# A decoder block's front: token rows summed at written-out points, a fourth place for split rows, and the final roots spread a step later

## The chip, the cores and the metric

The kernel runs on one core of a Trainium2 chip. The time is device microseconds of one execution, the median of the runs shown. The engines of a core work side by side, each in the order of its own queue: TensorE (PE, matrix products), VectorE (DVE), ScalarE (ACT), GpSimd (POOL) and SyncE (SP), whose queue issues nearly all transfers between the chip's memory and the core's.

## The reference

One layer on x of 2048 tokens by 1024 channels, in float32:

```
hn  = RMSNorm(x) * norm1_g
u_pool | q | k | v = hn @ W_in             # 512 channels each
y   = pool mixer(u_pool)                   # window means 2, 4, 8, 16, minus u; a 128x128 product each
o   = stick-breaking attention(q, k, v)    # 8 heads of 64 channels, causal
h   = x + [RMSNorm(y), RMSNorm(o)] @ W_out
h   = h + relu(RMSNorm(h) @ W_up)^2 @ W_down
out = RMSNorm(h) * final_g
```

## The kernel before

Channels lie on the 128 partitions, tokens along the free dimension, in four tiles of 512 tokens (`NT = 4`). To keep float32 accuracy every operand of a large product is split in a high and a low part (`split`, L150 and L151: ACT writes the rounded high part, DVE the rest), and each product is three matmuls (L182 to L184: high by high, high by low, low by high).

The kernel has a front (norm 1, input projection, pool mixer, attention), the output projection, the up projection and the down projection; the last two use a Strassen-like scheme with fewer block products. `front(q)` treats tiles 2q and 2q + 1, called a and b. It writes a program: steps (`in_proj`, one step for 128 output channels of one tile, 24 matmuls) and notes (Python calls between the steps). Output channels 0 to 3 are the pool groups, 4 to 7 q, 8 to 11 k, 12 to 15 v. In q = 0, tile 0's first ten projections come first, then six channel blocks for tiles 0 and 1 in turn with the same weights, then tile 1's last ten. Attention (`near`, units of two blocks of 128 queries) is spread among the steps.

Small work waits in a first-in first-out list, `later`. After each step `run` takes one or more entries of it (`catch_up`), and a note can empty it. What an entry issues on an engine is put behind certain earlier instructions of that engine, the last split of weights and the evacuation before the last. The instructions of each engine are otherwise ordered by a planner that runs when the kernel is built, with modelled times: ready work can be put ahead of work written earlier.

Norm 1 of tile 0 sums squares over the transposed tile. For tiles 1 to 3 (`norm1_rms(j)`) four blocks of 128 token rows of x, 128x1024 each, are loaded into a single buffer, tag `xr` in pool `pa`, and squared in place by ACT, which also accumulates each row's sum into `sums1`. Load and squares are entries of `later`; then come the inverse root on POOL and its spread over the partitions (`to_all`: eight matmuls at L248, a copy by ACT). For tile 1 the note stands before the fourth projection of tile 0, for tile 2 at the start of the shared blocks, for tile 3 at the start of q = 1.

The ring with the tag `st` (three places) holds split rows on their way to memory: `pls` (pool differences), `qk`, `vt` (v, transposed) and `mix` (the normed outputs). A place is free once its store has landed, or for `pls` once its matmuls are done. The constant tile `rlast`, 4 KB on each partition, holds two spread roots of norm 2, written in the up projection.

The down projection ends with the product P3, in two halves of eight steps, `kk` 0 to 7. Between steps the final norm of finished token tiles is done: `final_root` takes the means (eight matmuls at L210, a DVE instruction at L218) and makes the root on POOL, `yr`, in some 15 small instructions; `final_put` spreads it by eight matmuls (L248), ACT copies it, DVE multiplies eight chunks (L1403) and SP stores them (L1404). In the second half the steps 6 and 7 are held back for `last_steps`, which finishes the last token tile (stores at L1458).

Of the kernel before, what the change touches and what calls it, by code (L numbers as in the profile page):

```python
# [8 lines left out]
F32 = mybir.dt.float32  # L9
F32R = mybir.dt.float32r  # L10
# [5 lines left out]
P = 128  # L16
# [29 lines left out]
def hymba_block(ctx: ExitStack, tc: tile.TileContext, xT, x_rows, gains, w_in, pool_w, w_out, w_up, w_down, out):  # L46
# [259 lines left out]
        return (hpb if j % 2 else hpa).tile([P, 2, T], F32R, tag="h", name="h", align_bytes=256)  # L306

    def make_st():
        return pa.tile([P, 2, T], F32R, tag="st", name="mix", align_bytes=256, bufs=3)


    pw = []
# [15 lines left out]
    def note(emit):  # L328
        prog.append((0, emit, False))
# [39 lines left out]
    def norm1_first():  # L369
# [10 lines left out]
            ss = sum_squares([x[:, k] for k in range(KD)])  # L380
        st[0]["r"] = inv_rms(ss, D, root_tile(), nc.vector)

    def norm1_rms(j):
        got = st[j]["ss"] = sums1[:, j - 1]
        t = {}

        def load(b):
            t[b] = pa.tile([P, D], F32, tag="xr", name="xr", bufs=1)
            nc.sync.dma_start(t[b], x_rows[j, b])

        def square(b):
            nc.scalar.activation(t[b], t[b], AF.Square, accum_out=got[:, b:b + 1])
            if b + 1 < TB:
                load(b + 1)
        later.append(lambda: load(0))
        later.extend(lambda b=b: square(b) for b in range(TB))
        later_rms(st[j], "r", lambda: st[j]["ss"], D, lambda: root_tile() if j == 2 else None, j == 1)

    def norm1(j):
# [14 lines left out]
    def pool_group(j, g, ps):  # L414
        w = WINDOWS[g]
        if g == 0:
            st[j]["y"] = pa.tile([P, 4, T], F32, tag="yb", name="yb", bufs=1)
        u = pa.tile([P, PAD + T], F32, tag="u", name="u")
        nc.gpsimd.tensor_copy(u[:, 0:PAD], carry[:, g])
        if j == 0:  # L420
            took = nc.vector.tensor_tensor(u[:, PAD:], ps, st[0]["r"], ALU.mult)
        else:
            took = nc.scalar.activation(u[:, PAD:], ps, AF.Copy)
        nc.gpsimd.tensor_copy(carry[:, g], u[:, T:T + PAD])
        pl = pa.tile([P, T], F32, tag="ev", name="pl")
        if w == 2:
            nc.vector.tensor_tensor(pl, u[:, PAD - 1:PAD + T - 1], u[:, PAD:], ALU.subtract)
            if j == 0:
                nc.vector.tensor_tensor(pl[:, 0:1], u[:, PAD:PAD + 1], u[:, PAD:PAD + 1], ALU.subtract)
        else:  # L430
            sums = pa.tile([P, PAD + T], F32, tag="s", name="s")
            if w == 4:
                pair = pa.tile([P, PAD + T], F32, tag="s", name="s")
                nc.vector.tensor_tensor(pair[:, PAD - 2:], u[:, PAD - 2:], u[:, PAD - 3:PAD + T - 1], ALU.add)
                nc.vector.tensor_tensor(sums[:, PAD:], pair[:, PAD:], pair[:, PAD - 2:PAD + T - 2], ALU.add)
            else:
                nc.vector.tensor_tensor_scan(sums[:, PAD:], u[:, PAD:], u[:, PAD - w:PAD + T - w], window_sum[:, g:g + 1],
                                             op0=ALU.add, op1=ALU.subtract)
                if j < NT - 1:
                    nc.vector.tensor_reduce(window_sum[:, g:g + 1], u[:, PAD + T - w:], axis=mybir.AxisListType.X, op=ALU.add)  # L440
            nc.vector.scalar_tensor_tensor(pl, sums[:, PAD:], 1.0 / w, u[:, PAD:], op0=ALU.mult, op1=ALU.subtract)
            if j == 0:
                nc.vector.tensor_tensor(pl[:, 0:w - 1], sums[:, PAD:PAD + w - 1], recip[:, 0:w - 1], ALU.mult)
                nc.vector.tensor_tensor(pl[:, 0:w - 1], pl[:, 0:w - 1], u[:, PAD:PAD + w - 1], ALU.subtract)
        d = pa.tile([P, 2, T], F32R, tag="st", name="pls", align_bytes=256, bufs=3)
        split((d[:, 0], d[:, 1]), pl)
        pp = psx.tile([P, T], F32, tag="px", name="pp")
        nc.tensor.matmul(pp, pw[0][:, 0, g], d[:, 0], start=True, stop=False)
        nc.tensor.matmul(pp, pw[0][:, 0, g], d[:, 1], start=False, stop=False)
        nc.tensor.matmul(pp, pw[0][:, 1, g], d[:, 0], start=False, stop=True)  # L450
        nc.scalar.activation(st[j]["y"][:, g], pp, AF.Copy, scale=gs[:, g:g + 1])
        return took
# [16 lines left out]
        normed(4, part, g, make_st, lambda: st[j]["rm"], mx[j][at:at + 4])  # L469

    def keep_qk(j, c, dst, ps):
        d = pa.tile([P, 2, T], F32R, tag="st", name="qk", align_bytes=256, bufs=3)
        if j == 0:
            t = pa.tile([P, T], F32, tag="ev", name="qkr")
            nc.vector.tensor_tensor(t, ps, st[0]["r"], ALU.mult)
            ps = t
        took = split((d[:, 0], d[:, 1]), ps)
        for e in range(2):
            for x in range(2):
                nc.sync.dma_start(dst[2 * c + e][j][x * DH:(x + 1) * DH].bitcast(F32),  # L480
                                  d[e * DH:(e + 1) * DH, x].bitcast(F32))
        return took

    def keep_v(j, c, ps):
        vf = pa.tile([P, T], F32, tag="ev", name="vf")
        if j == 0:
            took = nc.vector.tensor_tensor(vf, ps, st[0]["r"], ALU.mult)
        else:
            took = nc.scalar.activation(vf, ps, AF.Copy)
        pt = psx.tile([P, TB, 2, DH], F32, tag="px", name="ptv")  # L490
        for b in range(TB):
            nc.tensor.transpose(pt[:, b], vf[:, b * P:(b + 1) * P], ident)
        vt = pa.tile([P, 2, TB, 2, DH], F32R, tag="st", name="vt", align_bytes=256, bufs=3)
        split((vt[:, :, :, 0], vt[:, :, :, 1]), pt.rearrange("p b e d -> p e b d"))
        for e in range(2):
            nc.sync.dma_start(vs[2 * c + e][j].bitcast(F32),
                              vt[:, e].rearrange("p b x d -> p (b x d)").bitcast(F32))
        return took
# [47 lines left out]
    def front(q):  # L546


        a, b = 2 * q, 2 * q + 1

        def rate(i):
            note(lambda: state.update(ratio=RATIO_FRONT[3 * q + i]))
        rate(0)
        if q == 0:
            note(start)
            note(norm1_first)
            note(pool_weights)
        else:
            note(lambda: (load_x(b, bigp), norm1_rms(b), norm1(b), pace(2)))
        for i, c in enumerate((EARLY if q else FIRST) + POOL):  # L560
            if q == 0 and i == 2:
                note(lambda: load_x(b, x0p))
            if q == 0 and i == 3:
                note(lambda: norm1_rms(b))
            if q == 0 and i == 4:
                note(lambda: (catch_up(len(later)), norm1(b)))
            if q == 0 and i == 8:
                note(lambda: (catch_up(len(later)), to_att(), load_x(b + 1, bigp)))
                attend(a, 0)
                attend(a, 1)  # L570
            in_proj(a, c)
            if q and i in (2, 5):
                attend(a, i // 3)
        note(lambda: (catch_up(len(later)), pool_norm(a)))
        rate(1)
        for h2 in (2, 3):
            note(lambda h2=h2: (norm1_rms(2) if h2 == 2 else None) if q == 0 else attn_norm(0) if h2 == 2 else None)
            for c in range(4 + h2, 16, 4):
                in_proj(a, c)
                in_proj(b, c, True)  # L580
            attend(a, h2)
            attend(b, h2)
        note(lambda: (catch_up(len(later)), (load_acc(0), load_mix(0, KD), attn_norm(1)) if q else norm1(b + 1), pace(1)))
        rate(2)
        for i, c in enumerate(EARLY + POOL if q else POOL + EARLY):
            if q == 0 and i == 4:
                note(lambda: pool_norm(b))
            if q == 0 and i == 6:
                note(lambda: pace(2))
            if q and i == len(EARLY):  # L590
                note(lambda: (catch_up(len(later)), pace(1)))
            in_proj(b, c)
            if i in ((2, 5) if q else (6, 9)):
                attend(b, i // 3 % 2 if q else i // 9)
        note(lambda: (catch_up(len(later)), (pool_norm(b), catch_up(len(later))) if q else None))
# [596 lines left out]
    def down(pools):  # L1192
# [320 lines left out]
        for g, (n_, i, kk, qs_) in enumerate(steps):  # L1513
# [26 lines left out]
            if n_ == "P3":  # L1540
                if qs_ == (1,):
                    free = 0
                if kk in (0, 2) and finals:
                    final_root(*finals.pop(0))
                elif kk in (1, 3) and roots:
                    final_put(*roots.pop(0))
                elif kk == 4 and qs_ == (1,):
                    last_turn()
        last_steps(held, PAIRS[1][0])
# [175 lines left out]
```

## Time and profile before

| | us |
|---|---|
| runs | 1877.05, 1880.71, 1885.54 |
| median | 1880.71 |
| profiled execution, its time | 1885.53 |
| profiled execution, its span from the first to the last instruction | 1883.8 |

The mean granted TensorE clock over the span is 0.995 of full speed. The profile is that of one execution; it names instructions by line, engine and tile, says how long each engine was busy, and puts each idle time of an engine down to what ended it.

### The profile page before, as it was taken

To read this page: it belongs to the slowest core of one execution; us is meant where nothing else is said; L and a number is where in the kernel's file an instruction comes from. 1 tells how busy PE (TensorE), PEld (TensorE's weight loads), DVE (VectorE), ACT (ScalarE), POOL (GpSimd) and SP (SyncE) were. 2 spreads that over 40 slices of the span, in tenths; PEclk is the share of its full clock that TensorE was granted. 3 is DMA by queue.
4 is the path that set the end of the run, shared out by engine and by line. 5 is a ranking of instruction groups with operands and counts; after the bars stand their busy time and mean duration, and the time that the engine had idled before them with its cause. 6 is when DMAs were issued, how large, how long until landed. Compare 5 with 4: busy or idle time off the path is not lost.

```text
span 1883.8 us, 26602 instructions
## 1 busy us (share of the span) xinstructions
PE 1861.4 (99%) x8859; PEld 1550.8 (82%) x8859; DVE 1457.0 (77%) x2100; ACT 1027.4 (55%) x1620; POOL 224.5 (12%) x466
## 2 busy tenths in 40 slices
PE   9999999999999999999999999999999999999997
PEld 7888878888888888888888888887888888888887
DVE  6977779677865977887799988886665677988774
ACT  6655667465544455555567555554332665656543
POOL 1222124122311040000000000000010010020110
PEclk9999999999999999999999999999999999999999
DMA  8876796899797868988798988889999899999862
GB/s 271 265 270 201 234 301 223 258 326 303 261 360 256 297 215 293 344 281 309 277 347 304 320 293 284 287 301 337 370 328 329 276 318 305 331 298 347 288 212 92
DMA packets 223892, 542.20 MB, mean 288 GB/s; under 512 B 26240, under 2 KB 32384, under 8 KB 219904
## 3 DMA queue, kind: packets, MB, share of 16 engines
q1 hardware_dynamic: 218992, 531.75, 81.2%
q0 software_dynamic: 4608, 8.39, 2.5%
q8 instruction: 72, 1.18, 0.3%
q14 instruction: 76, 0.62, 0.1%
q10 hardware_dynamic: 144, 0.26, 0.0%
HBM read 355.75 MB, written 184.55 MB: 287 GB/s over the span
## 4 chain that ended last, share of the span: by engine, by line
PE 79%; DMA 8%; DVE 7%; issue 2%; ACT 2%; POOL 1%; SPq 1%; DVEq 0%; ACTq 0%; POOLq 0%
PE pb L1349 16%; PE pY L1176 16%; PE pb L1527 12%; PE pZ L1176 8%; PE pd L182 6%; PE pd L183 6%; PE pd L184 6%; PE pX L1176 4%; PE po L730 1%; PE pta L718 1%; DVE hl L151 1%; DMA raw<-in_w_in_dram 1%; DMA t<-in_w_down_dram 1%; DMA sr<-su 1%; DMA h<-mx 1%
## 5 line engine op out<-in xcount | busy, mean ns | idle before, releaser
L1176 PE MATMUL pY<-sa,hw 128*128 128x512 f32 x1536 | 365.7, 389 | 0.8 <-ACT u L1099 0.7
L1176 PEld LDWEIGHTS pY<-sa,hw 128*128 128x128 f32 x1536 | 288.0, 188 | 61.8 <-ACT u L1099 1.3
L1349 PE MATMUL pb<-ad,wd 128*128 128x512 f32 x1344 | 305.1, 389 | 0.2 <-DVE ad L151 0.2
L182 PE MATMUL pd<-h,hl 128*128 128x512 f32 x752 | 296.9, 395 | 3.8 <-DVE qk L151 3.8
L183 PE MATMUL pd<-h,hl 128*128 128x512 f32 x752 | 296.6, 394 | 0.0
L184 PE MATMUL pd<-h,hl 128*128 128x512 f32 x752 | 296.0, 394 | 0.0
L1349 PEld LDWEIGHTS pb<-ad,wd 128*128 128x128 f32 x1344 | 252.2, 188 | 53.0 <-DVE ad L151 0.6
L1527 PE MATMUL pb<-ad,wd 128*128 128x512 f32 x1104 | 253.6, 390 | 1.4 <-ACT ad L150 1.3
L1527 PEld LDWEIGHTS pb<-ad,wd 128*128 128x128 f32 x1104 | 206.6, 188 | 44.8 <-ACT ad L150 1.8
L151 DVE TENSOR_TENSOR ad<-ar,ad 128x1024 fp32r<-128x1024 f32 x160 | 194.1, 1220 | 42.6 <-ACT ad L150 42.0
L150 ACT ACTIVATE ad<-ar 128x1024 fp32r<-128x1024 f32 x160 | 168.9, 1057 | 90.2 <-PE pb L1349 25.2
L1176 PE MATMUL pZ<-sa,hw 128*128 128x512 f32 x768 | 185.7, 389 | 0.0
L150 ACT ACTIVATE hl<-raw 128x512 fp32r<-128x512 f32 x168 | 104.0, 629 | 119.6 <-PE pd L184 73.2
L1176 PEld LDWEIGHTS pZ<-sa,hw 128*128 128x128 f32 x768 | 144.1, 188 | 29.8
L182 PEld LDWEIGHTS pd<-h,hl 128*128 128x128 f32 x752 | 141.9, 189 | 31.3 <-DVE qk L151 4.2
L184 PEld LDWEIGHTS pd<-h,hl 128*128 128x128 f32 x752 | 141.9, 189 | 28.4
L151 DVE TENSOR_TENSOR hl<-raw,hl 128x512 fp32r<-128x512 f32 x168 | 114.5, 687 | 65.6 <-ACT hl L150 65.1
L183 PEld LDWEIGHTS pd<-h,hl 128*128 128x128 f32 x752 | 142.0, 189 | 26.4
L151 DVE TENSOR_TENSOR hw<-rt,hw 128x512 fp32r<-128x512 f32 x128 | 86.5, 684 | 33.6 <-ACT hw L150 33.5
L150 ACT ACTIVATE wd<-wq 128x1024 fp32r<-128x1024 f32 x56 | 59.5, 1063 | 79.3 <-PE pb L1349 70.4
L151 DVE TENSOR_TENSOR wd<-wq,wd 128x1024 fp32r<-128x1024 f32 x56 | 68.4, 1222 | 37.3 <-ACT wd L150 35.8
L1093 ACT ACTIVATE a<-a 128x512 f32<-128x512 f32 x96 | 60.0, 629 | 65.4 <-DVE a L1135 29.3
(235 smaller groups left out, 2688.8 us busy)
## 6 DMA issues: line engine op xcount, KB each, us to landing
ar<-sd SPq DMA_DIRECT2D x96, 512.0 KB, 5.9
ar<-sdi SPq DMA_DIRECT2D x64, 512.0 KB, 5.7
rb<-in_w_up_dram SPq DMA_DIRECT2D x30, 1024.0 KB, 6.5
sd<-a SPq DMA_DIRECT2D x104, 256.0 KB, 5.1
raw<-in_w_in_dram SPq DMA_DIRECT2D x50, 512.0 KB, 4.6
sdi<-hr SPq DMA_DIRECT2D x96, 256.0 KB, 5.4
wr<-in_w_down_dram SPq DMA_DIRECT2D x48, 512.0 KB, 5.6
sd<-s SPq DMA_DIRECT2D x88, 256.0 KB, 4.6
```

What stands on the lines that cost most here:

```text
L150: nc.scalar.activation(hi, src, AF.Copy)
L151: return nc.vector.tensor_tensor(lo, src, hi.bitcast(F32), ALU.subtract)
L182: nc.tensor.matmul(ps, hl[:, 0, c], hi, start=(k == 0), stop=False)
L183: nc.tensor.matmul(ps, hl[:, 0, c], lo, start=False, stop=False)
L184: last_mm[0] = nc.tensor.matmul(ps, hl[:, 1, c], hi, start=False, stop=(k == n - 1))
L718: nc.tensor.transpose(pt[:, x * P:(x + 1) * P], sg[:, x * P:(x + 1) * P], ident)
L730: nc.tensor.matmul(po[0:m, p * 256 + to:p * 256 + to + hi - lo], vw[:, 2 * p + v, 0:m], at[:, x, lo:hi], start=(p == 0 and n == 0), skip_g ...
L1093: nc.scalar.activation(t, src, AF.Relu)
L1176: nc.tensor.matmul(t, w[:, wx, c], a[:, ax, c % 2], start=first and c == 0 and x == 0, stop=last and c == G - 1 and x == 2, skip_group_che ...
L1349: nc.tensor.matmul(b, t[:, wx, 2 * (kk % 2) + c, i * P:(i + 1) * P], a[:, ax, c], start=p in ("P1", "P5", "P2") and kk == 0 and c == 0 and ...
L1527: nc.tensor.matmul(ps[q, n], block(t, wx, c, n), left_[q][:, ax, c], start=(n_ in ("P1", "P3") and kk == 0 and c == 0 and x == 0), stop=(n ...
```

## The change

Four edits. The ring `st` gets a fourth place. The token rows' buffer `xr` goes; `rlast` takes its part. Loads and squares are written out by a generator, `row_sums`, in five parts per tile (load 0; square 0 and load 1; and so on; square 3), which notes call at written points and not through `later`: for tile 1 all five before tile 0's fifth projection, for tile 2 one before each of the first five shared blocks (the root follows at the sixth), for tile 3 one before every second of tile 1's last ten projections. And in P3 the spread of a root, with its multiplications and stores, comes after step 2 or 4 and no longer after 1 or 3; where both fall on step 2, the spread stands ahead of the next root.

```
     def make_st():
-        return pa.tile([P, 2, T], F32R, tag="st", name="mix", align_bytes=256, bufs=3)
+        return pa.tile([P, 2, T], F32R, tag="st", name="mix", align_bytes=256, bufs=4)
...
+    def row_sums(j):
+
+        x = rlast.rearrange("p x t -> p (x t)")
+        for b in range(TB + 1):
+            if b:
+                nc.scalar.activation(x, x, AF.Square, accum_out=sums1[:, j - 1, b - 1:b])
+            if b < TB:
+                nc.sync.dma_start(x, x_rows[j, b])
+            yield
+
+    row_steps = [iter(())] + [row_sums(j) for j in range(1, NT)]
+
+    def sum_rows(j, n=1):
+        for _ in range(n):
+            next(row_steps[j])
+
     def norm1_rms(j):
-        got = st[j]["ss"] = sums1[:, j - 1]
-        t = {}
-
-        def load(b):
-            t[b] = pa.tile([P, D], F32, tag="xr", name="xr", bufs=1)
-            nc.sync.dma_start(t[b], x_rows[j, b])
-
-        def square(b):
-            nc.scalar.activation(t[b], t[b], AF.Square, accum_out=got[:, b:b + 1])
-            if b + 1 < TB:
-                load(b + 1)
-        later.append(lambda: load(0))
-        later.extend(lambda b=b: square(b) for b in range(TB))
+        st[j]["ss"] = sums1[:, j - 1]
         later_rms(st[j], "r", lambda: st[j]["ss"], D, lambda: root_tile() if j == 2 else None, j == 1)
...
-            if q == 0 and i == 3:
-                note(lambda: norm1_rms(b))
             if q == 0 and i == 4:
-                note(lambda: (catch_up(len(later)), norm1(b)))
+                note(lambda: (sum_rows(b, TB + 1), norm1_rms(b), catch_up(len(later)), norm1(b)))
...
         for h2 in (2, 3):
-            note(lambda h2=h2: (norm1_rms(2) if h2 == 2 else None) if q == 0 else attn_norm(0) if h2 == 2 else None)
+            if q and h2 == 2:
+                note(lambda: attn_norm(0))
             for c in range(4 + h2, 16, 4):
+                if q == 0 and (h2, c) != (3, 15):
+                    note(lambda: sum_rows(2))
+                elif q == 0:
+                    note(lambda: norm1_rms(2))
                 in_proj(a, c)
                 in_proj(b, c, True)
...
         for i, c in enumerate(EARLY + POOL if q else POOL + EARLY):
+            if q == 0 and i % 2:
+                note(lambda: sum_rows(3))
...
+                if kk in (2, 4) and roots:
+                    final_put(*roots.pop(0))
                 if kk in (0, 2) and finals:
                     final_root(*finals.pop(0))
-                elif kk in (1, 3) and roots:
-                    final_put(*roots.pop(0))
                 elif kk == 4 and qs_ == (1,):
                     last_turn()
```

The other three uses of the tag `st` change `bufs=3` to `bufs=4` in the same way.

## Rows read from the trace of the kernel before

**Rows 1.** The page's first part: busy us, share, instructions of each engine.

```profile
PE 1861.4 (99%) x8859; PEld 1550.8 (82%) x8859; DVE 1457.0 (77%) x2100; ACT 1027.4 (55%) x1620; POOL 224.5 (12%) x466
```

**Rows 2.** Busy time by stretch: us, engines' busy us (instructions), clock, DMA share, GB/s.

```profile
12.00:40.00 28.00, 28.00 (x133) 23.47 (x132) 16.97 (x38) 17.98 (x33) 0.75 (x3) 1.00 0.81 293
...
1840.00:1884.00 44.00, 34.27 (x224) 30.77 (x222) 19.40 (x42) 16.67 (x31) 0.00 (x0) 0.91 0.27 99
```

**Rows 3.** PE's waits: who waited for whom, us in total, times, longest.

```profile
PE pd L182 <- DVE qk L151: 3.8, 2, 3.6
```

**Rows 4.** Busy time in stretches of 2 us, the same columns.

```profile
246.00:248.00 2.00, 0.00 (x0) 0.00 (x0) 2.00 (x4) 1.95 (x5) 0.00 (x0) 0.88 1.06 369
...
252.00:254.00 2.00, 2.00 (x6) 1.56 (x5) 0.16 (x1) 0.00 (x0) 0.00 (x0) 0.50 0.99 340
```

**Rows 5.** The chain that ended last, 225 to 262 us: start, us, what.

```profile
248.75 0.79 PE pd L182
249.54 0.43 PE pd L183
...
255.99 0.24 PE pd L183
```

**Rows 6.** ACT's timeline, 228 to 258 us: start, us, what, [idle before, what ended it].

```profile
240.11 1.06 ACT L392 ACTIVATE xr<-xr 128x1024 f32<-128x1024 f32 x1 [2.23 <-DMA xr<-in_x_rows_dram]
...
243.73 0.63 ACT L150 ACTIVATE mix<-nt 128x512 fp32r<-128x512 f32 x1 [1.50 <-DMA vs<-vt]
...
247.24 0.59 ACT L150 ACTIVATE qk<-pd 128x512 fp32r<-128x512 f32 x1
```

**Rows 7.** Busy time in the front by stretch, columns as in rows 2.

```profile
40.00:60.00 20.00, 20.00 (x98) 16.65 (x97) 16.15 (x28) 8.83 (x16) 5.35 (x16) 1.00 0.80 201
60.00:80.00 20.00, 19.80 (x90) 16.04 (x89) 19.87 (x37) 12.16 (x22) 8.37 (x7) 1.00 1.00 352
...
160.00:180.00 20.00, 20.00 (x107) 16.96 (x106) 14.97 (x24) 12.78 (x24) 5.11 (x7) 1.00 0.53 178
...
236.00:260.00 24.00, 20.40 (x102) 17.03 (x101) 16.21 (x24) 13.73 (x26) 3.52 (x7) 0.86 0.99 359
```

**Rows 8.** The tile xr: ns min/median/max, first and last start; then its readers' waits.

```profile
L389 SPq DMA_DIRECT2D xr<-in_x_rows_dram x12: 327/351/1117, 9.2 to 252.1; - x12
L392 ACT ACTIVATE xr<-xr x12: 1042/1058/1082, 16.6 to 259.6; 128x1024 f32<-128x1024 f32 x12
...
  DMA xr<-in_x_rows_dram: 10.2, 6
```

**Rows 9.** SP's timeline, issues of token rows.

```profile
39.02 0.33 SPq L389 DMA_DIRECT2D xr<-in_x_rows_dram  x1
...
233.58 0.37 SPq L389 DMA_DIRECT2D xr<-in_x_rows_dram  x1
```

**Rows 10.** Groups by line, 0 to 640 us: busy us, mean ns, idle before, releasers.

```profile
L150 ACT ACTIVATE mix<-nt 128x512 fp32r<-128x512 f32 x24 | 14.5, 630 | 7.5 <-DMA vs<-vt 6.5 <-DVE nt L296 0.8 <-DMA mx<-mix 0.2
```

**Rows 11.** Timelines of PE, POOL and SP in P3 and at the end.

```profile
1779.53 0.95 PE L210 MATMUL pm<-inv,ss 128*128 128x1 f32 x8
1789.67 0.33 PE L248 MATMUL pr<-identr,yr 128*128 128x128 f32 x1 [0.88 <-POOL yr L1394]
...
1789.70 0.20 POOL L1395 TENSOR_TENSOR yr<-v,yr 128x4 fp32r<-128x4 f32 x1
...
1805.04 0.20 POOL L1395 TENSOR_TENSOR yr<-v,yr 128x4 fp32r<-128x4 f32 x1
...
1844.48 2.32 SPq L1404 DMA_DIRECT2D out_dram<-p  x4
...
1871.43 6.47 SPq L1458 DMA_DIRECT2D out_dram<-res  x4
```

**Rows 12.** Timelines of ACT and PE, 52 to 64 us.

```profile
57.36 1.16 ACT L150 ACTIVATE hl<-raw 128x512 fp32r<-128x512 f32 x2 [4.50 <-DMA raw<-in_w_in_dram]
...
63.06 0.39 PE L182 MATMUL pd<-h,hl 128*128 128x512 f32 x1
```

More of the change, by code (lines that the diff above doesn't have):

```diff
@@ L444, in pool_group @@
                 nc.vector.tensor_tensor(pl[:, 0:w - 1], pl[:, 0:w - 1], u[:, PAD:PAD + w - 1], ALU.subtract)
-        d = pa.tile([P, 2, T], F32R, tag="st", name="pls", align_bytes=256, bufs=3)
+        d = pa.tile([P, 2, T], F32R, tag="st", name="pls", align_bytes=256, bufs=4)
         split((d[:, 0], d[:, 1]), pl)
@@ L471, in keep_qk @@
     def keep_qk(j, c, dst, ps):
-        d = pa.tile([P, 2, T], F32R, tag="st", name="qk", align_bytes=256, bufs=3)
+        d = pa.tile([P, 2, T], F32R, tag="st", name="qk", align_bytes=256, bufs=4)
         if j == 0:
@@ L492, in keep_v @@
             nc.tensor.transpose(pt[:, b], vf[:, b * P:(b + 1) * P], ident)
-        vt = pa.tile([P, 2, TB, 2, DH], F32R, tag="st", name="vt", align_bytes=256, bufs=3)
+        vt = pa.tile([P, 2, TB, 2, DH], F32R, tag="st", name="vt", align_bytes=256, bufs=4)
         split((vt[:, :, :, 0], vt[:, :, :, 1]), pt.rearrange("p b e d -> p e b d"))
```

## The prediction

> **What bounds the kernel now.** I read the page's first part, then who made TensorE (PE) wait, then the one stretch where the waits are, engine by engine. PE is busy for 1861.4 of 1883.8 us [rows 1]; its idle time is 22.4 us in all. No edit here removes PE work: the squares run on ScalarE (ACT), the root's spread keeps its eight small matmuls. So the change can only win what PE loses by waiting and by its clock, and can only lose by new waits. The last 44 us hold 9.7 us of that idle time [rows 2], from the last steps and stores, and part of the rest lies at the start, where the first operands are loaded; the change touches neither.
>
> The list of PE's waits has one large entry: 3.6 us in one piece, PE's matmul L182 for the vector engine's (DVE) split of a q or k tile [rows 3]. In two-microsecond windows PE has nothing at all from 246 to 248 us, and behind that the granted clock is 0.50, the lower of its two levels (1.2 GHz), still from 252 to 254 us [rows 4]. The chain shows what that costs: eleven matmuls from 249.54 us on stand 0.43 us apart where 0.23 is normal, and the one ahead of them takes 0.79 [rows 5]. That is 11 x 0.20 + 0.56, or 2.8 us, on top of the stall. The place costs 3.6 + 2.8 = 6.4 us.
>
> Why it waited is on ACT, which does its instructions in order. It stood 2.23 us for a load of x's token rows (xr), did that square, and a little later stood 1.50 us until a store (vs from vt) freed a place in the ring of split rows, tag st [rows 6]. The q/k split that PE needed was queued behind: ACT's half began at 247.24 us, and DVE's follows it. The 3.7 us of ACT's idling are nearly the 3.6 us of PE's. Both waits are on transfers, in a stretch where the 16 DMA engines are 0.99 busy [rows 7].
>
> **The change, part by part.**
> *Token rows, tile 3.* Before, the four loads and squares of tile 3 are entries of the queue `later` in the second half of the front. Its first load went out long before, as soon as tile 2 had left the buffer; the other three were issued from 233.58 to 252.1 us [rows 8, 9], with squares in between. Now they are written out in the loop over tile 1's last ten projections, some 160 to 222 us. The stretch 236 to 260 us loses the transfers of three loads (3 x 0.52 MB, at 359 GB/s 4.4 us) and three squares (1.06 us each, 3.2 us of ACT); the 2.23 us wait is gone. From 160 to 180 us the DMA engines are 0.53 busy [rows 7], so the loads fit there.
>
> *Token rows, tiles 1 and 2.* The same count of loads and squares, at other places. Tile 1's were already early (9 to 38 us). Over the 12 squares ACT waited 10.2 us for their loads, in 6 waits [rows 8]; only the one at 240 us reached PE. What these places cost is bounded by nothing below, since ACT is 55% busy [rows 1], and by one more event like that at 245 us above, 6.4 us. The nearest rows are those of tile 1's own squares: they lie before 39 us, with some of the six waits, and PE was busy throughout 12 to 60 us [rows 2, 7]. I take 0.
>
> *Fourth place in the ring.* Same bytes in all: xr's 4 KB per partition go, a place of 4 KB comes, since the rows now use `rlast`, which nothing else writes before the up projection. A split fills a place once the store three fills back has landed; now four back. ACT's waits on this before mix were 6.5 us in the front [rows 10], of which only the 1.50 us above is seen at PE. Its gain is in the 6.4 us already counted; beyond that I take 0. From below nothing: no instruction is added.
>
> *Roots spread one step later.* In P3 a root is begun after step 0 and spread over the partitions by PE after step 1. At 1789.67 us PE stood 0.88 us for GpSimd's (POOL) yr, which was whole at 1789.9 [rows 11]. A step of one half is 24 matmuls of 0.227 us, 5.45 us. After step 2 the spread is due at about 1779.5 + 1 + 2 x 5.45 = 1791.4, the mean's matmuls of 1779.5 counted as 1 us, when yr has been there for 1.5 us. Gain 0.9. The second root's mean passes DVE behind the eight multiplications of the first output, which come 1.7 us later now, so it is whole at about 1805.2 + 1.7 = 1807 [rows 11], against a place after step 4 at about 1779.5 + 4 x 5.45 + 3 = 1804. PE could wait there for up to 3 us if its order puts the spread right behind step 4. In the trace the first spread stood late among the matmuls of a later step than its place in the code, 9 us behind step 0 where step 1 ends after 6.5: the order kept it back until the root was nearly there, and I expect the same of the second: 0. The third spread comes at most one step, 5.45 us, later; its stores were issued from 1844.48 us, and the kernel's last ones go out from 1871.43 us [rows 11]. That gap of 27 us hides it; without it the 5.45 us would be added to the end.
>
> **Sum**, against the profiled execution's 1885.5 us: -3.6 - 2.8 - 0.9 = -7.3, so 1878.2 us, -0.4% of that execution. That execution is the slowest of the runs shown (1877.05, 1880.71, 1885.54), and the spread of 8.5 us is of the size of the stall: I read it as runs with and without it. A run without the stall should then be near 1877 to 1879 already, and against the median the gain is 2 to 3 us, 0.1 to 0.2%. I forecast **1878 us**: no change that can be told, half a per cent (9.4 us) being about what a measurement of this kernel can tell.
>
> **Rivals.**
> *The fixed points do not hold, and the rows come in a burst early.* Entries of `later` were made to stay behind an evacuation; the new squares are not, and the order within an engine follows readiness too: tile 2's first load, written behind ten projections of tile 0 (240 matmuls at 0.23 us, from 6 us on, so not before 60 us), went out at 39.02 us [rows 9]. Unheld, the eight pairs of tiles 2 and 3 could follow tile 1's at its pace, 39.0 - 9.2 = 29.8 us for four [rows 8, 9]: all between 39 and 99 us. Five loads more then fall between 40 and 80 us, 2.6 MB or 7.4 us of transfer at 352 GB/s, where 0.20 of 20 us, 4.0 us, is free [rows 7]; 3.4 us is pushed onto others, weights among them. There ACT waited 4.50 us for weights; the split it then began at 57.36 us (some 0.6 us on ACT, as much on DVE) is, by count, the one that the tenth projection uses from 63.06 us on [rows 12]: slack 4.5 us, just enough. This rival decides when pushed weights and a square's wait fall together and make it over 4.5 us late; two events at the price of 245 us then give 1878.2 + 12.8 = 1891, slower. The Trainium skill speaks for it: "DMA: Bandwidth & Descriptors", section "Queues, rings and completion order", says that each DMA engine takes descriptors in ring order, so a weight load issued behind a row load stands behind it. The rows agree as far as they go, ACT's 4.50 us ending when raw landed. By the fabric ceiling of 435 GB/s in the same page's Specifications the five loads would be an estimated 6 us instead of 7.4, 2 us over instead of 3.4. Chance of the burst with no event or one (1878 to 1885): inside the forecast's case; of two or more, slower: 0.08.
>
> *The stall only moves.* Without the three loads DMA would still be 0.99 - 4.4 / 24 = 0.81 busy from 236 to 260 us, since q, k, v and weights are fetched there, and a different order of ACT's and DVE's queues after 222 us may put another evacuation late. One event again: 1885.5 - 0.9 = 1884.6. Against it: 4.4 us less transfer and 3.2 us less of ACT in 24 us, and the fourth place. Chance 0.2.
>
> *More is won than I count.* PE's idle time apart from the end and what is counted is 22.4 - 9.7 - 3.6 - 0.9 = 8.2 us, the start's in it. If the fourth place and the quieter queues save 2 of them, it is 1876.2; all of them would give 1870. Being faster by over 0.5%, under 1871.3, needs nearly all, or a fast run (1877.05) less 6: 0.07.
>
> **How the numbers follow.** Forecast case (stall gone, nothing new, 1875 to 1880) 0.65; stall moved or one new event (1880 to 1886) 0.2; two or more new events 0.08; faster than 1871.3 0.07. The 8-in-10 range is 1872 to 1886: the lower end takes in the small waits and 3 us of run-to-run spread, the upper one event. By the bound of 0.5% the first two cases are both no change: 0.85, faster 0.07, slower 0.08.
>
> **What would show it.** Right: no PE wait over 1 us and no clock of 0.50 between 20 and 1870 us; no row load after 225 us; ACT's waits for stores before mix and qk smaller; no PE wait for POOL at the first spread. Wrong: loads of rows bunched at 40 to 100 us with hl splits late behind raw; a new 3 us wait of L182 with the lower clock behind it; a wait of L248 of 1 to 3 us at the second spread.

## The result, and the profile after

The changed kernel takes 1884.68 us in the median, the kernel before 1880.1 us beside it; the ratio is 1.0020, with a 95% interval of 1.0013 to 1.0027. So it is some 3.8 us slower, which the number of runs (22 of each; one of each, 4602.52 and 2058.55 us, lies far off the others and is not in the ratio) can tell, where 1878 us, a little faster, was forecast. The profiled execution of the changed kernel took 1886.55 us (span 1884.8), that of the kernel before 1885.53.

The page's first part after, beside [rows 1]: as much PE work, 1.0 us less of it busy.

```profile
PE 1860.4 (99%) x8859; PEld 1549.6 (82%) x8859; DVE 1458.4 (77%) x2100; ACT 1026.2 (54%) x1620; POOL 217.5 (12%) x466
```

PE's waits after, beside [rows 3]:

```profile
PE ptv L496 <- ACT vf L493: 3.9, 1, 3.9
PE pY L1185 <- ACT u L1108: 1.6, 1, 1.6
PE pzero L364 <- DVE zero L94: 1.5, 1, 1.5
```

The wait for a q or k split is gone. In its place stands one of 3.9 us for ACT's evacuation of v (`vf`), at another place. Busy time by stretch after, beside [rows 4] (the last two lines) and for the new place (the first two; columns as there):

```profile
120.00:125.00 5.00, 1.07 (x11) 0.93 (x10) 1.17 (x2) 2.34 (x5) 0.00 (x0) 0.77 0.80 267
125.00:130.00 5.00, 5.00 (x17) 4.24 (x16) 4.59 (x8) 2.99 (x7) 1.74 (x1) 0.55 0.49 175
246.00:248.00 2.00, 2.00 (x16) 1.78 (x16) 2.00 (x4) 1.29 (x3) 1.10 (x1) 1.00 1.06 393
252.00:254.00 2.00, 2.00 (x19) 1.87 (x18) 1.90 (x4) 1.09 (x3) 0.00 (x0) 1.00 0.98 313
```

Near 247 us PE is busy at the full clock, as forecast. Between 120 and 130 us it now does what it did near 247 us before the change: it stands, and then runs at the lower of the clock's two levels (1.2 GHz; 0.55 over five microseconds). The token rows' tile after, beside [rows 8] (columns as there):

```profile
L390 SPq DMA_DIRECT2D rlast<-in_x_rows_dram x12: 327/339/812, 8.6 to 119.3; - x12
L388 ACT ACTIVATE rlast<-rlast x12: 1041/1061/1101, 16.7 to 123.0; 128x1024 f32<-128x1024 f32 x12
...
  DMA rlast<-in_x_rows_dram: 22.8, 8
```

All twelve loads and squares are done by 124 us, though tile 3's are written in a loop that begins behind 160 us: the points of the code do not hold them. The last four, from 102 to 123 us, are tile 3's. ACT's waits for them grew from 10.2 to 22.8 us. ACT's timeline, 100 to 128 us, shows the last three; PE's shows when the matmuls that `vf` is made from ended, and when PE got `vf`:

```profile
113.45 1.06 ACT L388 ACTIVATE rlast<-rlast 128x1024 f32<-128x1024 f32 x1 [7.30 <-DMA rlast<-in_x_rows_dram]
...
118.17 1.06 ACT L388 ACTIVATE rlast<-rlast 128x1024 f32<-128x1024 f32 x1 [3.08 <-DMA rlast<-in_x_rows_dram]
...
122.99 1.06 ACT L388 ACTIVATE rlast<-rlast 128x1024 f32<-128x1024 f32 x1 [2.66 <-DMA rlast<-in_x_rows_dram]
123.95 0.19 ACT L388 ACTIVATION_READ_ACCUMULATOR rlast<-rlast 128x1 f32 x1
124.04 0.58 ACT L493 ACTIVATE vf<-pd 128x512 f32<-128x512 f32 x1
```

```profile
116.73 0.40 PE L184 MATMUL pd<-h,hl 128*128 128x512 f32 x1
...
124.67 1.12 PE L496 MATMUL ptv<-ident,vf 128*128 128x128 f32 x4 [3.93 <-ACT vf L493]
```

The chain that ended last, 118 to 132 us, names the link between two squares: with one buffer a load can only be issued when the square before it is done.

```profile
114.63 3.52 DMA rlast<-in_x_rows_dram
...
119.14 0.19 ACT rlast L388
119.33 0.02 issue
119.35 3.62 DMA rlast<-in_x_rows_dram
...
124.14 0.49 ACT vf L493
```

To put prices on places I timed PE's way through the front in every profile: from one of its matmuls into the tile pd (the projections' sums) to a later one, counted from the first (a projection has 24). In us:

```
                 288 to 384   384 to 480   768 to 864   864 to 1152   ratio to before
before               32.63        30.42        36.87        90.17
before, again        32.39        30.43        35.43        90.17
changed              34.27        36.30        31.38        90.61         1.0020
```

In the changed kernel the third stretch holds eight matmuls L248 more (0.9 us), which before are in the fourth. For equal work it is thus 30.5 against 36.87, and the fourth 91.5 against 90.17: the stretch with the old stall loses 6.4 us, the one at 117 to 153 us takes 5.9 more, and the two others 1.6 and 1.3 more.

The roots: the wait for the first spread is gone, and the second and third come 11.9 and 9.1 us after their means, as before (12.1 and 9.1), without a wait. PE's timeline in P3 after, beside [rows 11]:

```profile
1781.68 0.95 PE L210 MATMUL pm<-inv,ss 128*128 128x1 f32 x8
1793.49 1.00 PE L248 MATMUL pr<-identr,yr 128*128 128x128 f32 x8
1794.34 1.00 PE L210 MATMUL pm<-inv,ss 128*128 128x1 f32 x8
1806.28 1.28 PE L248 MATMUL pr<-identr,yr 128*128 128x128 f32 x8
1834.02 0.95 PE L210 MATMUL pm<-inv,ss 128*128 128x1 f32 x8
1843.12 0.22 PE L248 MATMUL pr<-identr,yr 128*128 128x128 f32 x1
```

### The profile page after: what moved, and what is told of

It reads as the page before. It is cut to its first block, busy times and chain, and to the rows that moved or that the text cites. A ratio compares the mean times of both kernels' runs of the same rounds, so it can differ in the third digit from the quotient of the medians.

```text
span 1884.8 us, 26582 instructions
## 1 busy us (share of the span) xinstructions
PE 1860.4 (99%) x8859; PEld 1549.6 (82%) x8859; DVE 1458.4 (77%) x2100; ACT 1026.2 (54%) x1620; POOL 217.5 (12%) x466
## 4 chain that ended last, share of the span: by engine, by line
PE 78%; DMA 9%; DVE 7%; ACT 2%; issue 2%; SPq 1%; POOL 0%; DVEq 0%; ACTq 0%; POOLq 0%
PE pY L1185 16%; PE pb L1358 14%; PE pb L1536 12%; PE pZ L1185 8%; PE pd L182 6%; PE pd L184 6%; PE pd L183 6%; PE pX L1185 4%; PE po L739 1%; DMA ar<-sd 1%; PE pta L727 1%; DMA rlast<-in_x_rows_dram 1%; DMA xt<-in_xT_dram 1%; DMA t<-in_w_down_dram 1%; DVE hl L151 1%
```

## The experiments

Theory A: the squares of tiles 2 and 3 are held by nothing, run in a burst behind tile 1's, and ACT stands for each load, at the end long enough to stop PE. Theory B: the fourth place of the ring costs. Theory C: the end pays for the roots. Later A2, a rival inside A: not ACT's standing but the crowd of transfers before 125 us costs.

**Each part alone.** First the token rows on the kernel before (rows_alone: three places, roots as before; the diff is that of `row_sums`):

> Only the token rows change: generator, squares in rlast, ring of three places, roots as before. Theory A (the squares of tiles 2 and 3, no longer held behind anything, run in a burst right after tile 1's, ACT stands for their loads, and PE stalls near 123 us with the lower clock behind it): a wait of PE of about 4 us between 100 and 130 us, no stall near 245 us, and a ratio to the kernel before of 1.002 to 1.005, at least that of the whole change (1.002), since the gain of the roots is missing. Theory B (the fourth place of the ring, which lets more stores run at a time, is what costs): no stall near 123 us, ratio 0.997 to 1.000.

Ratio 1.0011 (1.0002 to 1.0021). PE waited 2.6 us for `vf`, near 122 us, with the lower clock behind it; ACT waited 21.1 us for rows. No stall near 247 us: the stretch 768 to 864 takes 31.41 us, 384 to 480 takes 34.32. The place and the sign are theory A's; the ratio is below the range it gave and above theory B's.

```profile
PE ptv L496 <- ACT vf L493: 2.6, 1, 2.6
```

**The ring alone** (ring_only), with the row loads in their old queue; the other three uses of the tag change likewise:

```
-        return pa.tile([P, 2, T], F32R, tag="st", name="mix", align_bytes=256, bufs=3)
+        return pa.tile([P, 2, T], F32R, tag="st", name="mix", align_bytes=256, bufs=4)
...
-            t[b] = pa.tile([P, D], F32, tag="xr", name="xr", bufs=1)
+            t[b] = rlast.rearrange("p x t -> p (x t)")
```

> Only the ring gets its fourth place; the row loads stay in the queue they were in, but use rlast so that the memory suffices. Theory A: ACT's waits for stores before mix and qk shrink, the stall near 245 us is shorter or gone, ratio 0.998 to 1.000. Theory B: ratio 1.002 to 1.004, with new waits of PE in the front.

Ratio 0.9995 (0.9986 to 1.0004). The stall near 247 us is gone, with the row squares still there (768 to 864: 30.94 us; 384 to 480: 30.38). Theory B falls. But the next stretch, 864 to 1152, takes 93.10 us where it took 90.17: between 300 and 320 us PE is now busy 18.24 of 20, in small waits at the full clock. Some 2.9 us of what the place wins are given back there.

```profile
300.00:320.00 20.00, 18.24 (x101) 14.42 (x100) 19.60 (x29) 12.31 (x24) 11.46 (x14) 1.00 0.74 253
236.00:260.00 24.00, 24.00 (x141) 20.53 (x139) 18.57 (x27) 16.90 (x33) 5.29 (x12) 1.00 0.98 345
```

**The roots alone** (roots_only):

```
+                if kk in (2, 4) and roots:
+                    final_put(*roots.pop(0))
                 if kk in (0, 2) and finals:
                     final_root(*finals.pop(0))
-                elif kk in (1, 3) and roots:
-                    final_put(*roots.pop(0))
```

> Only the spreads of the roots move a step later. Both theories: PE's 0.9 us for the first spread is gone, no new wait at the second, 0.9 to 2.8 us less (the traces show 2.8 us gained between 1749 and 1805 us), ratio 0.9985 to 0.9995. Theory C (the end pays for the later stores): ratio 1.000 or above, with the last stores issued later by what the first spread gained.

Ratio 0.9997 (0.9988 to 1.0007): within the interval no change, and 0.6 us less as its middle. The wait for POOL is gone. The last stores were not held up: the third spread stands 9.1 us behind its mean in either kernel, since the order had already put it behind a later step. Theory C has nothing for it. This kernel's front is that of the kernel before, and has its stall again, with 2.1 us of waiting:

```profile
PE pd L182 <- DVE qk L151: 2.1, 1, 2.1
```

**The squares of tiles 2 and 3 held** in the changed kernel (held23). The code takes ACT's last split of any kind, not the weights' alone:

```
     def split(dst, src):
         hi, lo = dst
-        nc.scalar.activation(hi, src, AF.Copy)
+        last_hi[0] = nc.scalar.activation(hi, src, AF.Copy)
...
-                nc.scalar.activation(x, x, AF.Square, accum_out=sums1[:, j - 1, b - 1:b])
+                with tc.issue_after(last_hi[0].ins) if j > 1 else nullcontext():
+                    nc.scalar.activation(x, x, AF.Square, accum_out=sums1[:, j - 1, b - 1:b])
```

> The changed kernel, but the squares of tiles 2 and 3 are each put behind the weight split that ACT was last given when they are written, so they run where they are written and not in a burst. Theory A: no ACT wait of over 3 us for a row load, no PE stall near 123 us, none near 245 us, ratio to the kernel before 0.996 to 0.999. Theory B: ratio stays near 1.002, since the fourth place is still there.

Ratio 0.9982 (0.9973 to 0.9992), faster than both kernels with nothing else changed. The rows now run from 8.6 to 213.7 us, ACT waits 5.4 us for them, twice, and there is no PE wait over 1.6 us in the whole trace (from 120 to 130 us and from 236 to 260 us PE is busy throughout, at the full clock).

```profile
120.00:130.00 10.00, 10.00 (x59) 8.51 (x58) 9.58 (x16) 7.36 (x15) 2.80 (x4) 1.00 0.77 237
236.00:260.00 24.00, 24.00 (x146) 20.87 (x144) 22.32 (x34) 15.32 (x30) 5.40 (x6) 1.00 0.98 332
```

```profile
L393 SPq DMA_DIRECT2D rlast<-in_x_rows_dram x12: 328/336/383, 8.6 to 213.7; - x12
...
  DMA rlast<-in_x_rows_dram: 5.4, 2
```

**Rows and ring together, roots put back** (rows_ring), to see whether the parts only add:

> The changed kernel with the roots put back: token rows and fourth place together. Its front has the order of the changed kernel. Theory A (the burst costs, whatever the ring does): a PE wait of 2.5 to 4 us near 123 us behind ACT's waits for row loads, ratio 1.0015 to 1.0025. Theory A1 (run-to-run luck made the changed kernel's 3.9 us, the burst being worth what the rows alone gave): ratio 1.000 to 1.001, a wait of about 2.6 us or less. Theory B (rows and ring only add): 1.0011 - 0.0005 = 1.0006.

Ratio 1.0018 (1.0008 to 1.0028), a PE wait of 4.8 us, 37.03 us from 384 to 480. So the changed kernel's 3.9 us were no accident. Whether rows and ring add is left open: 1.0006 is the sum of two ratios that are each known to about 0.001, and 1.0018 is within that. The waits were longer with four places (4.8 and 3.9 us) than with three (2.6), but these are one profile each, and the old stall measured 2.1 to 3.6 us in three profiles of one front. That four places make the burst dearer is not shown.

```profile
PE ptv L496 <- ACT vf L493: 4.8, 1, 4.8
```

**One tile held at a time** (held3 and held2: `j == 3`, and `j == 2`, in the edit above):

> The changed kernel with the squares of tile 3 alone held where they are written; tile 2's run right behind tile 1's, as in the changed kernel. Theory A3 (it is the last squares of the burst, tile 3's, which follow one another with nothing between, that make ACT stand and PE stall near 123 us): no PE wait over 2 us in the front, ratio 0.998 to 0.999, as with both held. Theory A2 (tile 2's, at 43 to 104 us, cost as much, through the transfers): ratio 0.9995 to 1.001.

> The changed kernel with the squares of tile 2 alone held; tile 3's follow tile 2's at once. Theory A3 (squares that follow one another with nothing between cost wherever they stand): a PE wait of 2 to 4 us at 140 to 165 us, ratio 1.000 to 1.002. Theory A2 (only the crowd of transfers before 125 us costs): ratio 0.998 to 0.999, no such wait.

0.9986 (0.9977 to 0.9995) and 0.9987 (0.9977 to 0.9997). With tile 3 held, ACT's waits for rows are 10.7 us and the stretch 384 to 480 takes 29.96 us: the end of the burst, tile 3's squares, is what cost. (One other place lost time in that profile: 288 to 384 takes 34.82 us, where PE waited 0.8 us for DVE and the lower clock followed.) With tile 2 held, tile 3's squares follow at once, to 168 us; ACT waited 4.60 and 3.36 us for two of them, and still no PE wait over 0.5 us followed in the front. The second half of what is called A3 there, that a burst costs wherever it stands, is not borne out.

Nor is it enough that an evacuation stands right behind the waiting square: behind the 3.36 us stood `vf`, as in the changed kernel, and PE waited 0.28 us for it. What differs is how late `vf` came. From the start of the last matmul that it is made from to its own start it took 3.75 us here, 5.98 in rows_alone, 7.31 in the changed kernel and 8.23 in rows_ring; PE waited 0.28, 2.62, 3.93 and 4.85 us. Each wait is the lateness less 3.4 to 3.5 us: from that matmul's start on PE had other work for some 4.0 us, and `vf` itself takes 0.6.

```profile
154.10 1.06 ACT L391 ACTIVATE rlast<-rlast 128x1024 f32<-128x1024 f32 x1 [4.60 <-DMA rlast<-in_x_rows_dram]
161.56 1.06 ACT L391 ACTIVATE rlast<-rlast 128x1024 f32<-128x1024 f32 x1 [3.36 <-DMA rlast<-in_x_rows_dram]
...
162.62 0.58 ACT L496 ACTIVATE vf<-pd 128x512 f32<-128x512 f32 x1
```

```profile
158.87 0.39 PE L186 MATMUL pd<-h,hl 128*128 128x512 f32 x1
...
163.25 0.66 PE L499 MATMUL ptv<-ident,vf 128*128 128x128 f32 x4 [0.28 <-ACT vf L496]
```

**Two row buffers** (rows_two), on the rows alone; load b + 2 is issued behind square b:

```
-        x = rlast.rearrange("p x t -> p (x t)")
+        x = {}
+
+        def load(b):
+            x[b] = pa.tile([P, D], F32, tag="xr", name="xr", bufs=1) if b % 2 else rlast.rearrange("p x t -> p (x t)")
+            nc.sync.dma_start(x[b], x_rows[j, b])
+
+        load(0)
         for b in range(TB + 1):
             if b:
-                nc.scalar.activation(x, x, AF.Square, accum_out=sums1[:, j - 1, b - 1:b])
-            if b < TB:
-                nc.sync.dma_start(x, x_rows[j, b])
+                nc.scalar.activation(x[b - 1], x[b - 1], AF.Square, accum_out=sums1[:, j - 1, b - 1:b])
+            if b + 1 < TB:
+                load(b + 1)
             yield
```

> The rows alone, on the kernel before, with two row buffers in turn, so that a load is under way while ACT does the square before it; the squares still run in a burst, by the order as built even earlier. Theory A (ACT standing for a load is what costs): ACT's waits for row loads, 22.8 us in 8 in the changed kernel, fall to under 10, no PE wait over 1.5 us near 100 to 130 us, ratio 0.998 to 1.000. Theory A2 (the crowd of transfers between 40 and 125 us costs, by late weights): ratio 1.001 or more, with PE or the weight splits waiting for raw.

Ratio 0.9981 (0.9971 to 0.9990). This burst is denser and earlier, its last square at 80.7 us, and costs nothing: ACT waits 2.9 and 0.2 us for rows, once each. A2 falls with it, for the transfers are all there: from 40 to 80 us the DMA engines are 0.93 and 1.01 busy (0.80 and 1.00 in [rows 7]) and PE does not stop. At 245 us, the old place, PE still waited 1.1 us for a q or k split in this profile.

```profile
40.00:60.00 20.00, 20.00 (x98) 16.69 (x97) 16.53 (x28) 11.78 (x22) 1.86 (x2) 1.00 0.93 291
60.00:80.00 20.00, 20.00 (x95) 16.74 (x94) 19.69 (x38) 14.11 (x26) 5.93 (x10) 1.00 1.01 362
```

```profile
  DMA rlast<-in_x_rows_dram: 2.9, 1
...
  DMA xr<-in_x_rows_dram: 0.2, 1
```

**The faster parts together, the fourth place among held rows, and the kernel before once more.**

> Two row buffers in turn (ring of three places) and the roots spread a step later: the two parts that were faster, together. If they add: 0.9981 x 0.9997 = 0.9978, within 0.9970 to 0.9988. If the order of the front decides alone: as rows_two, 0.998. If the whole is luck of the order: anything from 0.997 to 1.001.

Two buffers (three places) and the later roots (two_roots): 0.9977 (0.9967 to 0.9987), median 1875.3 us. The best of these kernels, ahead of the kernel before and of the changed one; that it beats rows_two (0.9981) is inside the intervals.

> Squares of tiles 2 and 3 held, roots later, but three places in the ring: what the fourth is worth where the rows are held. Held with four was 0.9982. Theory A (the hold does it, the fourth place little): 0.998 to 0.999. If the fourth place is what takes the stall near 245 us away: a PE wait of 2 us or more there, ratio 0.999 to 1.001.

0.9986 (0.9977 to 0.9995) against 0.9982 with four places: no difference that these runs tell. With three places, too, PE waited no longer than 0.5 us near 245 us.

> The kernel before once more. If the stall near 245 us is part of every execution: a PE wait of over 2 us there with the lower clock behind it, of another size than 3.6 us. If it was an accident of the first profile: none.

1878.27 us in the one run of before_look, and the stall is there, with 3.2 us of waiting and the lower clock behind it:

```profile
PE pd L182 <- DVE qk L151: 3.2, 1, 3.2
```

```profile
248.00:250.00 2.00, 2.00 (x6) 1.51 (x6) 0.69 (x1) 0.78 (x3) 0.11 (x1) 0.50 1.03 419
```

## Why the prediction was wrong

**The stall near 245 us: right, and somewhat smaller than counted.** Its cause was read rightly, and either cure is enough: without the rows there (rows_alone) or with the fourth place (ring_only) it is gone; 1.1 us of waiting is the most that came back (rows_two). Its price of 6.4 us was that of one execution. In three profiles of that front (before, before_look, roots_only) the stretch took 36.87, 35.43 and 34.40 us against 30.5 for the same work without a stall: 6.4, 4.9 and 3.9, 5.1 in the mean. It is not a thing of some runs, as the sum read it: all three profiles have it, and the two of the kernel before differ by 7.3 us in their spans but by 1.4 us in this stretch. So the median most likely holds about 5 us of it, and a cure was worth 5 us against the median, not 2 to 3. held23 and rows_two, 0.0018 and 0.0019 faster (3.4 and 3.6 us), come near that.

**The step that failed** is the place of tile 3's rows, "written out in the loop over tile 1's last ten projections, some 160 to 222 us", and with it the cost of the rows' new places, "I take 0". Nothing held tile 3's rows: their squares ran from 102 to 123 us, at the end of a burst. That the points might not hold was the first rival, but the sum priced the new places at 0, because tile 1's own squares had waited on loads without harm. They were poor neighbours to price it by: PE did not stop there, whatever stood behind those squares, while at 124 us `vf`, which PE's transposes needed, was held up by two waiting squares for longer than PE had other work. The term measured 5.9 us at that place, against 0 taken and 6.4 as the bound given. Beside it the profile of the changed kernel has 1.6 and 1.3 us more, but rows_ring, with the same front, has only some 0.3 and 0.1 there (and 6.6 at the place), so these are not shown to be the burst's. The balance of the places by the profiles, -5.1 for the old stall and -0.9 for the spread against 5.9 + 1.6 + 1.3, is +2.8, and the ratio says 3.8.

**The burst was the right rival with the wrong price.** It was priced through weights made late by crowded transfers, with two events needed. Nothing of the kind occurred: rows_two has the crowd and no cost, and the weight split that waited 4.50 us in [rows 12] waited 4.48 us there, while from 12 to 300 us PE waited at most 0.3 us for such a split (0.4 in the changed kernel). ACT's standing for the loads is what cost, and one event was enough to undo the gain. The Trainium skill's rule on descriptors in ring order ("DMA: Bandwidth & Descriptors", section "Queues, rings and completion order") spoke for that way; the rule is not refuted here, but it did not decide, since the split had the slack. The burst also took longer than by tile 1's pace: its last square is at 123.0 us, not 99.

**"The stall only moves"** gave 1884.6 us, and 1884.68 was measured. That is luck, for the number came about in another way than it argued: the stall went to 124 us with the rows, and not to a neighbour of 245 us by crowded transfers.

**Roots and ring:** the wait for the first spread went, as said, and no second one came; 0.9 us was expected and 0.6 us measured, with an interval that holds 0. The third spread, for which up to 5.45 us were allowed, did not move at all. The fourth place won what it was credited with, and gave 2.9 us of it back from 864 to 1152, which the sum had at 0. Half a per cent was taken as the least that can be told of this kernel; 22 runs of each told 0.2%.

## What to carry to other kernels

Work taken out of a queue that held it does not stay where it is written: before pricing a move, find in the trace a piece that nothing held (here one load, issued 20 us and more ahead of its place) and follow that for all of them. Price a wait in an in-order engine by what stands behind the waiting instruction and by how long the engine that needs it has other work (4.0 us here), not by whether a similar wait was harmless elsewhere. Where an engine must square or copy what one buffer is loaded into, a second buffer, or a hold behind something late, was worth more here than choosing the place of the code.

## What the runs showed of the hardware

A wait of PE of 2.1 us was already followed by the lower clock: in roots_only the granted clock was 0.50 from 248 to 250 us behind it. So a stall's price there was 1.5 to 1.9 times its length: 3.9 us for 2.1 of waiting, 4.9 for 3.2, 6.4 for 3.6. The length of the wait alone does not tell whether the clock falls: in held3 a wait of 0.8 us at 100.5 us was followed by 0.50 as well, while the changed kernel's wait of 1.0 us at 110 us was not.

```profile
248.00:250.00 2.00, 2.00 (x6) 1.55 (x5) 0.70 (x2) 0.60 (x1) 0.00 (x0) 0.50 1.03 418
```

held3:

```profile
102.00:104.00 2.00, 2.00 (x12) 1.90 (x11) 2.00 (x5) 1.95 (x5) 1.36 (x4) 0.50 0.98 318
```

The half-megabyte row loads of the changed kernel took from 3.5 to 9.9 us from issue to landing (median 6.0), against 3.6 to 7.1 (median 5.9) in the kernel before.
